# Padding two small tiles, a common ring for the spilled MLP blocks, and priorities for two short chains in a hybrid decoder layer

## The chip, the cores and the metric

The kernel runs on one core of one Trainium2 chip. A core has TensorE (PE in the profile; its weight loads are PEld), VectorE (DVE), ScalarE (ACT), GpSimd (POOL) and SyncE (SP), and 16 DMA engines; DMAs are issued by SP, ACT and POOL, each in the order of its own queue. The metric is the device time of one execution in microseconds.

## What is computed

One decoder layer on 512 rows of 1024 columns, all in float32. Cut to what matters:

```python
u = rms_norm(h, norm_mix_g)
conv_in, c_q, c_kv, k_rope_raw, gate_logits = split(u @ w_in)
conv_out = conformer_conv(conv_in, ...)           # 31 taps, layer norm, silu, @ w_conv_out
mla_out = mla_attention(c_q, c_kv, k_rope_raw, ...)  # rms_norm of both latents, 8 causal heads
gates = sigmoid(gate_logits)
h = h + (gates[0] * conv_out + gates[1] * mla_out) @ w_out
h = h + memory_cross_attention(rms_norm(h), rms_norm(mem), ...)
h = h + square(relu(rms_norm(h) @ w_mlp1)) @ w_mlp2
return rms_norm(h, final_norm_g)
```

## The kernel before

Every float32 operand of a product is split into a high part, rounded to the format `fp32r`, and a low rest, and a product is three: high by high, high by low, low by high (`mm3`, lines 237 to 239). `prep` makes the two parts of a weight block, `wh` on ScalarE (line 202) and `wl` on VectorE or GpSimd (line 203); a `Pipe` calls it one unit ahead of the products. Most products are 128x128 weights by 512 columns; in `w_mlp1`, `w_out`, `w_in` and the heads the moving operand is an activation (`hgh`, `mgh`, `uh`, `yh`, `cqh`) and the weights are `wh` and `wl`; in the second MLP product and for the values it is the other way round, and `hA`, `hB` or `ckh` or `mh` are loaded as the weights while `wh`, `wl` or `xh`, `xl` move.

The instructions of TensorE stay in the order of the code (`manual_schedule`). A planner orders those of the other engines when the program is built: it takes what is ready by its own clock, and among several the one traced first; `tc.high_priority()` moves the instructions of a block to the front of that choice.

The stages in order of time: convolution inputs (`ag`), the query latent (`cq`), gates 0 to 5, the key and value latent (`ckv`), gates 6 to 15; the convolution's 124 taps run on VectorE beside them (line 494). Then values and heads, `mla_out`, `w_out` with `mem_norm`, the memory's keys, queries and values, the cross-attention, `w_xo`; the first MLP product (`m1_unit`), 32 units; the second, in seven passes (`PASSES`) of four chunks with 24 products each: a Strassen scheme on halves of the rows and columns, for which blocks `a11` to `s4` are made beside the first product.

*Memory.* Tiles are put on two stacks in the on-chip memory, from the bottom (pools `cst`, `sm`, `w`, `g`, `hg`, `xa`, `o`, `m2`, ...) and from the top (`y`, `lat`, `u`, `att`, `h`, `xm`, `mg`, `mlp`, ..., those with `side="right"`). `cst` lies at the bottom, and `paced` (line 1364) is one of its tiles; `rm` (line 909) is one of `xm`'s. Nearly all larger tiles are whole multiples of 256 bytes in a partition, so a small one decides where all that come after it stand. In the compiled kernel `wh`, `wl`, `xh`, `xl`, `hgh`, `hgl`, `oh`, `xoh` and `xpt` begin 32 bytes past a multiple of 256; `uh`, `ul`, `cqh`, `yh`, `ckh`, `vh`, `q`, `k`, `hA` and `hB` 224; `mh`, `xkh`, `xvh` and `mgh` 160.

*Row factors.* `latent_rows` (line 673) takes the sums of squares of a latent's four row blocks, makes a factor for each row by `rsqrt` (12 short instructions on VectorE) and scales the rows out of the PSUM banks. Gates are evacuated by line 725 from the same kind of bank, `mm`, of which there are four; two hold a latent until it is scaled.

*Spilled blocks.* The blocks `s3` and `a22` (`SPILLED`) are written to DRAM by line 1250, each chunk after its four row blocks are made, and read back by `reload` on ScalarE's queue; the two names have two buffers each. `s3` is used in pass 5, `a22` in pass 6 (counted from 0).

Of the kernel before, what the change touches and what calls it, by code (L numbers as in the profile page):

```python
# [14 lines left out]
F32 = mybir.dt.float32  # L15
# [4 lines left out]
ALU = mybir.AluOpType  # L20
# [3 lines left out]
P = 128  # L24
D = 1024
S = 512
NT = S // P
# [12 lines left out]
EPS = 1e-6  # L40
# [128 lines left out]
def _body(tc, a):  # L169
    nc = tc.nc  # L170
    dma = nc.sync.dma_start
    pe = nc.tensor
    dve = nc.vector
    act = nc.scalar
    gps = nc.gpsimd

    def pool(name, bufs=1, side=None, space=None):
        kw = dict(name=name, bufs=bufs, reuse_waits="tile")
        if side:
            kw["side"] = side  # L180
        if space:
            kw["space"] = space
        cm = tc.tile_pool(**kw)
        return cm, cm.__enter__()
# [5 lines left out]
    cst_cm, cst = pool("cst")  # L190
    sm_cm, sm = pool("sm", bufs=2)
# [4 lines left out]
    def bank(tag="mm"):  # L196
        nonlocal ps
        return ps.tile([P, S], F32, tag=tag, name=tag, bufs=PB[tag])


    def split(hi, lo, src, eng=None):
        act.copy(hi, src)  # L202
        (eng or dve).tensor_tensor(lo, src, hi.bitcast(F32), op=ALU.subtract)  # L203

    def split_scaled(hi, lo, src, scale):
        act.activation(hi, src, AF.Copy, scale=scale)
        dve.scalar_tensor_tensor(lo, src, scale, hi.bitcast(F32), op0=ALU.mult, op1=ALU.subtract)
# [23 lines left out]
    def mm3(out, pairs, first=True, last=True, again=False):  # L231

        n = len(pairs)
        cols = out.shape[-1] / S
        for i, ((wh, wl), (ah, al)) in enumerate(pairs):
            kw = dict(skip_group_check=True) if again else {}
            pe.matmul(out, wh, ah, start=first and i == 0, stop=False, **kw)  # L237
            pe.matmul(out, wh, al, start=False, stop=False, **kw)  # L238
            pe.matmul(out, wl, ah, start=False, stop=last and i == n - 1, **kw)  # L239
            tick(cols)  # L240

    def rsqrt(dst, v, n):
        t = sm.tile([P, n], F32, tag="rs_t", name="rs_t")
        ti = sm.tile([P, n], I32, tag="rs_i", name="rs_i")
        dve.tensor_scalar(ti, v.bitcast(I32), 1, None, op0=ALU.logical_shift_right)
        dve.tensor_scalar(dst.bitcast(I32), ti, -1, 0x5F3759DF, op0=ALU.mult, op1=ALU.add)
        for _ in range(3):
            dve.scalar_tensor_tensor(t, dst, -0.5, dst, op0=ALU.mult, op1=ALU.mult)  # L248
            dve.tensor_tensor(t, t, v, op=ALU.mult)
            dve.scalar_tensor_tensor(dst, t, 1.5, dst, op0=ALU.add, op1=ALU.mult)  # L250
# [10 lines left out]
    rx = cst.tile([P, NT], F32, name="rx")  # L261
    rx2 = cst.tile([P, NT], F32, name="rx2")
# [71 lines left out]
    def lhs(hl, k, m0=0, m=128):  # L334
        return hl[0][:, k, m0:m0 + m], hl[1][:, k, m0:m0 + m]
# [97 lines left out]
    n = NT * 16  # L433
# [239 lines left out]
    def latent_rows(bs, dim, cn):  # L673
        ss = sm.tile([P, NT], F32, tag="ss", name="ss")
        for t in range(NT):
            junk = wkp.tile([P, S], F32, tag="sg", name="junk")
            act.activation(junk[:, :dim], bs[t][:, :dim], AF.Square, accum_out=ss[:, t:t + 1])
        v = sm.tile([P, NT], F32, tag="rv", name="rv")
        dve.scalar_tensor_tensor(v, ss, 1.0 / dim, rx2, op0=ALU.mult, op1=ALU.mult)
        dve.tensor_scalar(v, v, EPS, None, op0=ALU.add)  # L680
        r = sm.tile([P, NT], F32, tag="rr", name="rr")
        rsqrt(r, v, NT)
        dve.tensor_tensor(r, r, rx, op=ALU.mult)
        for t in range(NT):
            act.activation(cn[:, t, :dim], bs[t][:, :dim], AF.Copy, scale=r[:, t:t + 1])

# [68 lines left out]
    def qkt(tag):  # L755
        return at.tile([P, 2, S], F32R, tag=tag, name=tag, bufs=QB)
# [4 lines left out]
    def prep_q(p):  # L761
        return prep(("uq", p // 2), c0=256 * (p % 2), cols=256)

    def q_head(hl, h):
        b = bank()
        e = h % 2
        mm3(b, [(lhs(hl, k, 128 * e), (cqh[:, k, :], cql[:, k, :])) for k in range(3)])
        t = at.tile([P, S], F32, tag="qtmp", name="qtmp", bufs=1)
        dve.tensor_tensor(t, b, tq[:, e, :], op=ALU.mult)
        q = qkt("q")  # L770
        split(q[:, 0, :], q[:, 1, :], t)
        qs[h] = q
# [66 lines left out]
    hq = None  # L839
    k_pair(0)  # L840
    for t in range(NT):
# [3 lines left out]
        split(vh[:, t, :], vl[:, t, :], b)  # L845
        if t == 0:
            hq = prep_q(0)
    q_head(hq, 0)
    q_head(hq, 1)
    hqs = {0: hq}  # L850

# [48 lines left out]
    xm_cm, xmp = pool("xm", side="right")  # L900
# [5 lines left out]
    ml = xmp.tile([P, KD, MEM], F32R, name="ml")  # L906
    rbm = xmp.tile([P, MEM], F32, name="rbm")

    rm = xmp.tile([P, 16], F32, name="rm")
    mg_cm, mgp = pool("mg", side="right")  # L910
    mgh = mgp.tile([P, KD, S], F32R, name="mgh")
    mgl = mgp.tile([P, KD, S], F32R, name="mgl")
# [256 lines left out]
    HT = S // 2  # L1169
    ml_cm, mlp = pool("mlp", side="right")  # L1170
    hop_cm, hop = pool("hop")
    blocks = {}
# [11 lines left out]
    def block(name, c):  # L1184

        if (name, c) not in blocks:
            if name in SPILLED:
                blocks[name, c] = mlp.tile([P, 4, HT], F32, tag="sp_" + name, name="sp_" + name, bufs=2)
            else:
                t = pair_tile(name, c // 2, (2, 4))  # L1190
                blocks[name, c // 2 * 2], blocks[name, c // 2 * 2 + 1] = t[:, 0], t[:, 1]
        return blocks[name, c]


    SPILLED = ("s3", "a22")
    asp = {(n, c): spp.tile([P, 4 * HT], F32, name="%s_%d" % (n, c)) for n in SPILLED for c in range(4)}

    def reload(name, c):
        t = mlp.tile([P, 4, HT], F32, tag="sp_" + name, name="re_" + name, bufs=2)
        act.dma_start(out=t.rearrange("p k m -> p (k m)"), in_=asp[name, c])  # L1200
        blocks[name, c] = t

    m2w = {}
# [8 lines left out]
    def v3(t):  # L1212
        return t.rearrange("p (k m) -> p k m", k=4)
# [76 lines left out]
    def split_h(name, c):  # L1290
        hi = mlp.tile([P, 4, HT], F32R, tag="hA", name="hA", bufs=2)
        lo = mlp.tile([P, 4, HT], F32R, tag="hB", name="hB", bufs=2)
        src = block(name, c)
        if name == "a22":
            split_scaled(hi, lo, src, -1.0)
        else:
            split(hi, lo, src)
        return hi, lo

    def split_w(src):  # L1300
        out = []
        for u in range(2):
            w = whl4(2, S)
            split(w[0], w[1], src[:, 2 * u:2 * u + 2, :])
            out.append(w)
        return out
# [54 lines left out]
    def add_to(t, what, c):  # L1361
        gps.dma_start(out=t, in_=hbm(what, c), accum_op=ALU.add, max_dma_last_dim=8192)

    paced = cst.tile([P, 16], F32, name="paced")

    def pace(lo):

# [15 lines left out]
    def load_v(c):  # L1383
        vs[c] = flat(pair_tile(("a12", "s1")[c // 2], c % 2, (1, 1)))
        dma(out=vs[c], in_=hbm("b22", c))
# [87 lines left out]
    def pass_unit(n, c):  # L1473
        aname, bk, again = PASSES[n]
        end = n == len(PASSES) - 1

        def prep_():
            if aname in SPILLED:
                for cc in {0: (0, 1), 3: ()}.get(c, (c + 1,)):
                    reload(aname, cc)  # L1480
            src, nxt = w_source(n, c)
            h, w = split_h(aname, c), split_w(v3(src))
            if n == 0 and c >= 2:
                load_b21(c - 2)
            if n == 1 and c < 2:
                load_b21(2 + c)
            if n == 2:
                load_v(c)
            if nxt:
                add_to(src, nxt, c)  # L1490
            if n == 1:

                with tc.issue_after(pace(w[0][1])):
                    add_to(xs[c], "b12", c)
            return h, w

        def main(hw):
            h, w = hw
            if c == 0 and not again:
                acc_[bk] = [bank("at" if bk in "bd" else "mm") for _ in range(2)]  # L1500
            if end and c == 2:
                held["hw"] = hw
            elif end and c == 3:
                for t in range(2):
                    part(acc_[bk][t], t, *held["hw"], False, False, again)
                    part(acc_[bk][t], t, h, w, False, True, again)
                    DONE[n](t)
            elif c in (0, 3):
                for t in range(2):
                    part(acc_[bk][t], t, h, w, c == 0 and not again, c == 3, again)  # L1510
                    if c == 3:
                        DONE[n](t)
            else:
                chunk(acc_[bk], h, w, c, again)
            if n == 0 and c == 0:
                late_pools()
                load_x(3)
            if n == 2 and c == 0:
                m2w["gf"] = w_tile(m2w["p"], "b21", "gf")[:, :D]
                dma(out=m2w["gf"], in_=a["gfin"].to_broadcast([P, D]))  # L1520
        pipe.unit(prep_, main)
# [32 lines left out]
```

## Time and profile before

| | us |
|---|---|
| median of 3 runs | 774.58 (774.38 to 774.97) |
| the profiled execution | 775.09 |
| its span, first to last instruction | 773.2 |
| TensorE busy | 756.4 (98% of the span) |
| VectorE busy | 525.3 (68%) |
| ScalarE busy | 399.9 (52%) |
| GpSimd busy | 76.4 (10%) |
| granted clock of TensorE, mean | 0.997 of 2.4 GHz |

A row of a timeline gives an instruction's start and duration, its engine and line, the tiles it writes and reads (for a product: bank, moving operand, weights), shapes, how many, and in brackets how long the engine was idle before it and what ended that. The duration of a product includes its way through the array, so two products overlap; how fast they follow each other is read from their starts.

### The profile page before, as it was taken

To read this page: it belongs to the slowest core of one execution; us is meant where nothing else is said; L and a number is where in the kernel's file an instruction comes from. 1 tells how busy PE (TensorE), PEld (TensorE's weight loads), DVE (VectorE), ACT (ScalarE), POOL (GpSimd) and SP (SyncE) were. 2 spreads that over 40 slices of the span, in tenths; PEclk is the share of its full clock that TensorE was granted. 3 is DMA by queue.
4 is the path that set the end of the run, shared out by engine and by line. 5 is a ranking of instruction groups with operands and counts; after the bars stand their busy time and mean duration, and the time that the engine had idled before them with its cause. 6 is when DMAs were issued, how large, how long until landed. Compare 5 with 4: busy or idle time off the path is not lost.

```text
span 773.2 us, 9487 instructions
## 1 busy us (share of the span) xinstructions
PE 756.4 (98%) x3594; PEld 623.8 (81%) x3594; DVE 525.3 (68%) x855; ACT 399.9 (52%) x681; POOL 76.4 (10%) x64
## 2 busy tenths in 40 slices
PE   8999999999999999999999999999999999999896
PEld 5889788777788887889888888888888888888784
DVE  6899999845888859756686634233333567666895
ACT  7234333478667537344474635444344565656562
POOL 0144426320000000000000000000000011111000
PEclk9999999999999999999999999999999999999998
DMA  8323123222103144333321434334353499999731
GB/s 277 111 95 111 58 95 127 73 77 96 56 0 110 56 154 165 116 110 110 109 109 54 164 108 152 136 132 182 108 209 117 148 291 263 278 216 212 197 109 54
DMA packets 26989, 103.36 MB, mean 134 GB/s; under 512 B 2368, under 2 KB 9920, under 8 KB 17984
## 3 DMA queue, kind: packets, MB, share of 16 engines
q1 hardware_dynamic: 13600, 67.54, 24.4%
q0 software_dynamic: 2304, 16.78, 10.5%
q10 hardware_dynamic: 11040, 18.45, 6.8%
q8 instruction: 28, 0.46, 0.2%
q14 instruction: 17, 0.14, 0.1%
HBM read 94.37 MB, written 8.39 MB: 133 GB/s over the span
## 4 chain that ended last, share of the span: by engine, by line
PE 80%; DVE 13%; DMA 3%; ACT 2%; issue 1%; SPq 0%; DVEq 0%; ACTq 0%
PE mm L239 21%; PE mm L238 21%; PE mm L237 21%; DVE cv L494 6%; PE at L238 4%; PE at L237 3%; PE at L239 3%; DMA re_s<-s 1%; PE at L816 1%; DVE wl L203 1%; PE at L797 1%; DVE rs_t L248 1%; DMA xr<-xT 1%; PE at L798 1%; PE at L795 1%
## 5 line engine op out<-in xcount | busy, mean ns | idle before, releaser
L202 ACT CAST wh<-raw 128x1024 fp32r<-128x1024 f32 (+4 forms) x103 | 102.7, 998 | 176.9 <-PE mm L238 148.7
L203 DVE TENSOR_TENSOR wl<-raw,wh 128x1024 fp32r<-128x1024 f32 (+3 forms) x77 | 90.7, 1178 | 106.7 <-ACT wh L202 106.4
L237 PE MATMUL mm<-hgh,wh 128*128 128x512 f32 x288 | 113.1, 393 | 0.0
L239 PE MATMUL mm<-hgh,wl 128*128 128x512 f32 x288 | 112.3, 390 | 0.0
L238 PE MATMUL mm<-hgl,wh 128*128 128x512 f32 x288 | 112.2, 389 | 0.0
L494 DVE SCALAR_TENSOR_TENSOR cv<-zpad,vec,cv 128x512 f32<-128x512 f32 x116 | 80.4, 744 | 0.1
L237 PE MATMUL mm<-uh,wh 128*128 128x512 f32 x176 | 70.8, 402 | 1.8 <-DVE sg L725 1.8
L239 PE MATMUL mm<-uh,wl 128*128 128x512 f32 x176 | 69.6, 395 | 0.1
L238 PE MATMUL mm<-ul,wh 128*128 128x512 f32 x176 | 69.5, 395 | 0.0
L203 POOL TENSOR_TENSOR wl<-raw,wh 128x1024 fp32r<-128x1024 f32 (+2 forms) x26 | 56.4, 2169 | 107.7 <-ACT wh L202 102.9
L239 PEld LDWEIGHTS mm<-hgh,wl 128*128 128x128 f32 x288 | 54.1, 188 | 11.4
L237 PEld LDWEIGHTS mm<-hgh,wh 128*128 128x128 f32 x288 | 54.1, 188 | 10.9
L238 PEld LDWEIGHTS mm<-hgl,wh 128*128 128x128 f32 x288 | 54.1, 188 | 10.9
L1368 POOL COPY paced<-wl 128x1 f32<-128x1 f32 x4 | 2.5, 615 | 468.2 <-DVE wl L203 468.2
L203 DVE TENSOR_TENSOR wl<-x,wh 128x1024 fp32r<-128x1024 f32 x25 | 30.4, 1222 | 19.3 <-ACT wh L202 18.6
L237 PEld LDWEIGHTS mm<-uh,wh 128*128 128x128 f32 x176 | 33.0, 188 | 11.0 <-issue 3.8
L238 PE MATMUL at<-wl,hA 128*128 128x512 f32 x96 | 37.9, 395 | 2.4 <-DVE wl L203 2.4
L239 PEld LDWEIGHTS mm<-uh,wl 128*128 128x128 f32 x176 | 33.0, 188 | 8.5 <-DVE wl L203 0.6
L238 PEld LDWEIGHTS mm<-ul,wh 128*128 128x128 f32 x176 | 33.1, 188 | 7.3
L202 ACT CAST wh<-x 128x1024 fp32r<-128x1024 f32 x25 | 26.1, 1047 | 24.6 <-PE at L239 9.6
L237 PE MATMUL at<-wh,hA 128*128 128x512 f32 x96 | 37.6, 392 | 0.0
L239 PE MATMUL at<-wh,hB 128*128 128x512 f32 x96 | 37.4, 390 | 0.0
(392 smaller groups left out, 1717.3 us busy)
## 6 DMA issues: line engine op xcount, KB each, us to landing
raw<-weights SPq DMA_DIRECT2D x42, 1024.0 KB, 4.8
x<-weights POOLq DMA_DIRECT2D x12, 1024.0 KB, 14.7
a<-weights SPq DMA_DIRECT2D x5, 1024.0 KB, 9.7
x<-weights SPq DMA_DIRECT2D x4, 1024.0 KB, 5.1
raw<-weights SPq DMA_DIRECT2D x4, 768.0 KB, 4.2
xr<-xT SPq DMA_DIRECT2D x8, 256.0 KB, 6.2
raw<-weights SPq DMA_DIRECT2D x4, 512.0 KB, 5.0
ht<-xT ACTq DMA_DIRECT2D x1, 2048.0 KB, 9.2
```

Source lines behind the costliest of these rows:

```text
L202: act.copy(hi, src)
L203: (eng or dve).tensor_tensor(lo, src, hi.bitcast(F32), op=ALU.subtract)
L237: pe.matmul(out, wh, ah, start=first and i == 0, stop=False, **kw)
L238: pe.matmul(out, wh, al, start=False, stop=False, **kw)
L239: pe.matmul(out, wl, ah, start=False, stop=last and i == n - 1, **kw)
L248: dve.scalar_tensor_tensor(t, dst, -0.5, dst, op0=ALU.mult, op1=ALU.mult)
L494: dve.scalar_tensor_tensor(run if w < CW - 1 else acc[:, c, :], zs, wcol, run, op0=ALU.mult, op1=ALU.add)
L795: pe.matmul(b[:, :n], q[:, 0, sl], k[:, 0, :n], start=True, stop=False)
L797: pe.matmul(b[:, :n], q[:, 0, sl], k[:, 1, :n], start=False, stop=False)
L798: pe.matmul(b[:, :n], q[:, 1, sl], k[:, 0, :n], start=False, stop=True)
L816: pe.transpose(b[:, (t - k) * P:(t - k + 1) * P], ptok[h, t][:, k * P:(k + 1) * P], ident)
L1368: return gps.tensor_copy(paced[:, 0:1], lo[:, 0, 0:1].bitcast(F32)).ins
```

## The change

Two tiles of 16 columns become 64 columns wide. The row factors of a latent and the instructions of the first query head get priority. The blocks `s3` and `a22` share one ring of four buffers, and reloads are issued from SP: all four chunks of `s3` at the second chunk of pass 4, and a chunk of `a22` behind the split of each chunk of `s3` in pass 5.

```diff
--- before.py
+++ after.py
@@ -675,12 +675,14 @@
         for t in range(NT):
             junk = wkp.tile([P, S], F32, tag="sg", name="junk")
             act.activation(junk[:, :dim], bs[t][:, :dim], AF.Square, accum_out=ss[:, t:t + 1])
-        v = sm.tile([P, NT], F32, tag="rv", name="rv")
-        dve.scalar_tensor_tensor(v, ss, 1.0 / dim, rx2, op0=ALU.mult, op1=ALU.mult)
-        dve.tensor_scalar(v, v, EPS, None, op0=ALU.add)
-        r = sm.tile([P, NT], F32, tag="rr", name="rr")
-        rsqrt(r, v, NT)
-        dve.tensor_tensor(r, r, rx, op=ALU.mult)
+
+        with tc.high_priority():
+            v = sm.tile([P, NT], F32, tag="rv", name="rv")
+            dve.scalar_tensor_tensor(v, ss, 1.0 / dim, rx2, op0=ALU.mult, op1=ALU.mult)
+            dve.tensor_scalar(v, v, EPS, None, op0=ALU.add)
+            r = sm.tile([P, NT], F32, tag="rr", name="rr")
+            rsqrt(r, v, NT)
+            dve.tensor_tensor(r, r, rx, op=ALU.mult)
         for t in range(NT):
             act.activation(cn[:, t, :dim], bs[t][:, :dim], AF.Copy, scale=r[:, t:t + 1])
 
@@ -845,7 +847,8 @@
         split(vh[:, t, :], vl[:, t, :], b)
         if t == 0:
             hq = prep_q(0)
-    q_head(hq, 0)
+    with tc.high_priority():
+        q_head(hq, 0)
     q_head(hq, 1)
     hqs = {0: hq}
 
@@ -906,7 +909,7 @@
     ml = xmp.tile([P, KD, MEM], F32R, name="ml")
     rbm = xmp.tile([P, MEM], F32, name="rbm")
 
-    rm = xmp.tile([P, 16], F32, name="rm")
+    rm = xmp.tile([P, 64], F32, name="rm")
     mg_cm, mgp = pool("mg", side="right")
     mgh = mgp.tile([P, KD, S], F32R, name="mgh")
     mgl = mgp.tile([P, KD, S], F32R, name="mgl")
@@ -1185,7 +1188,7 @@
 
         if (name, c) not in blocks:
             if name in SPILLED:
-                blocks[name, c] = mlp.tile([P, 4, HT], F32, tag="sp_" + name, name="sp_" + name, bufs=2)
+                blocks[name, c] = mlp.tile([P, 4, HT], F32, tag="sp", name="sp_" + name, bufs=4)
             else:
                 t = pair_tile(name, c // 2, (2, 4))
                 blocks[name, c // 2 * 2], blocks[name, c // 2 * 2 + 1] = t[:, 0], t[:, 1]
@@ -1196,8 +1199,8 @@
     asp = {(n, c): spp.tile([P, 4 * HT], F32, name="%s_%d" % (n, c)) for n in SPILLED for c in range(4)}
 
     def reload(name, c):
-        t = mlp.tile([P, 4, HT], F32, tag="sp_" + name, name="re_" + name, bufs=2)
-        act.dma_start(out=t.rearrange("p k m -> p (k m)"), in_=asp[name, c])
+        t = mlp.tile([P, 4, HT], F32, tag="sp", name="re_" + name, bufs=4)
+        dma(out=t.rearrange("p k m -> p (k m)"), in_=asp[name, c])
         blocks[name, c] = t
 
     m2w = {}
@@ -1361,7 +1364,7 @@
     def add_to(t, what, c):
         gps.dma_start(out=t, in_=hbm(what, c), accum_op=ALU.add, max_dma_last_dim=8192)
 
-    paced = cst.tile([P, 16], F32, name="paced")
+    paced = cst.tile([P, 64], F32, name="paced")
 
     def pace(lo):
 
@@ -1475,11 +1478,13 @@
         end = n == len(PASSES) - 1
 
         def prep_():
-            if aname in SPILLED:
-                for cc in {0: (0, 1), 3: ()}.get(c, (c + 1,)):
-                    reload(aname, cc)
+            if n == 4 and c == 1:
+                for cc in range(4):
+                    reload("s3", cc)
             src, nxt = w_source(n, c)
             h, w = split_h(aname, c), split_w(v3(src))
+            if aname == "s3":
+                reload("a22", c)
             if n == 0 and c >= 2:
                 load_b21(c - 2)
             if n == 1 and c < 2:
```

## Rows read from the trace of the kernel before

**Rows 1.** The page: busy us (share of the span) and instructions of each engine.

```profile
PE 756.4 (98%) x3594; PEld 623.8 (81%) x3594; DVE 525.3 (68%) x855; ACT 399.9 (52%) x681; POOL 76.4 (10%) x64
```

**Rows 2.** Waits of TensorE: us in total, times, longest.

```profile
PE at L238 <- DVE wl L203: 2.4, 1, 2.4
PE mm L237 <- DVE sg L725: 1.8, 2, 1.0
...
PE at L795 <- ACT q L202: 1.0, 1, 1.0
```

**Rows 3.** Timeline, TensorE, first MLP product: start, us, line, tiles, [idle].

```profile
504.69 0.39 PE L238 MATMUL mm<-hgl,wh 128*128 128x512 f32 x1
...
505.85 0.39 PE L237 MATMUL mm<-hgh,wh 128*128 128x512 f32 x1
...
515.14 0.40 PE L239 MATMUL mm<-hgh,wl 128*128 128x512 f32 x1
```

**Rows 4.** Timeline, TensorE, gate products, first and last of 66 starts.

```profile
120.69 0.40 PE L238 MATMUL mm<-ul,wh 128*128 128x512 f32 x1
...
135.86 0.39 PE L237 MATMUL mm<-uh,wh 128*128 128x512 f32 x1
```

**Rows 5.** Timeline, TensorE, `w_out`, first and last of 71 starts.

```profile
311.69 0.40 PE L237 MATMUL mm<-mgh,wh 128*128 128x512 f32 x1
...
327.95 0.40 PE L238 MATMUL mm<-mgl,wh 128*128 128x512 f32 x1
```

**Rows 6.** Timeline, TensorE, memory values, first and last of 30 starts.

```profile
393.13 0.40 PE L237 MATMUL mm<-wh,mh 128*128 128x512 f32 x1
...
399.87 0.39 PE L239 MATMUL mm<-wh,ml 128*128 128x512 f32 x1
```

**Rows 7.** Table of stretches: us, busy us (instructions) by engine, clock, DMA share, GB/s.

```profile
33.20:120.20 87.00, 85.94 (x440) 74.38 (x439) 86.98 (x141) 31.76 (x56) 36.57 (x18) 1.00 0.24 84
120.60:137.40 16.80, 16.11 (x70) 12.64 (x68) 16.76 (x29) 4.33 (x7) 9.56 (x12) 1.00 0.36 126
640.00:728.00 88.00, 88.00 (x386) 72.23 (x385) 61.92 (x66) 49.79 (x58) 11.49 (x14) 1.00 1.01 239
```

**Rows 8.** Timeline, VectorE, around the two latents.

```profile
74.53 0.35 DVE L679 SCALAR_TENSOR_TENSOR rv<-ss,rx 128x4 f32<-128x4 f32 x1
74.80 0.74 DVE L494 SCALAR_TENSOR_TENSOR cv<-zpad,vec,cv 128x512 f32<-128x512 f32 x1
...
77.65 2.11 DVE L248 SCALAR_TENSOR_TENSOR rs_t<-rr 128x4 f32<-128x4 f32 x1
...
88.02 0.68 DVE L725 TENSOR_TENSOR sg<-mm,rbx 128x512 f32<-128x512 f32 x1
...
120.64 0.31 DVE L679 SCALAR_TENSOR_TENSOR rv<-ss,rx 128x4 f32<-128x4 f32 x1 [0.46 <-ACT junk L677]
...
136.63 0.68 DVE L725 TENSOR_TENSOR sg<-mm,rbx 128x512 f32<-128x512 f32 x1
```

**Rows 9.** Timeline, VectorE, row factors of `mem_norm`.

```profile
310.50 0.15 DVE L248 SCALAR_TENSOR_TENSOR rs_t<-rm 128x2 f32<-128x2 f32 x1
310.57 0.48 DVE L207 SCALAR_TENSOR_TENSOR ml<-mr,vec,mh 128x256 fp32r<-128x256 f32 x1
310.96 0.15 DVE L249 TENSOR_TENSOR rs_t<-rs_t,rv 128x2 f32<-128x2 f32 x1
```

**Rows 10.** Timeline, VectorE, first query head.

```profile
194.38 1.23 DVE L203 TENSOR_TENSOR wl<-raw,wh 128x1024 fp32r<-128x1024 f32 x1 [0.39 <-ACT wh L202]
195.52 0.69 DVE L769 TENSOR_TENSOR qtmp<-mm,tq 128x512 f32<-128x512 f32 x1
```

**Rows 11.** Timeline, ScalarE, third `s3` chunk.

```profile
715.51 0.33 ACTq L1200 DMA_DIRECT2D re_s<-s  x1
...
726.89 1.05 ACT L202 CAST hA<-re_s 128x1024 fp32r<-128x1024 f32 x1 [3.09 <-DMA re_s<-s]
```

**Rows 12.** Timeline, VectorE, third `s3` chunk.

```profile
727.98 1.23 DVE L203 TENSOR_TENSOR hB<-re_s,hA 128x1024 fp32r<-128x1024 f32 x1 [1.89 <-ACT hA L202]
```

## The prediction

> **What bounds the kernel now.** I read the page first: TensorE has work in 756.4 of 773.2 us, 98% [rows 1]. So a gain has to come from one of two places: TensorE standing still, or its products following each other more slowly than they could. The list of waits gives the first: 2.4 us once on `wl`, 1.8 us in two pieces on `sg`, 1.0 us on `q` [rows 2], about 5 us in all; what else it holds is small or in the start-up. The second I read in the timeline from the starts of consecutive products of one shape (128x128 weights, 512 columns). In the first MLP product 41 intervals from 505.85 to 515.14 us make 9.29 us, 0.2266 us each [rows 3]. In the gate products 65 make 15.17, 0.2334 each [rows 4]; in `w_out` 70 make 16.26, 0.2323 [rows 5]; in the memory values 29 make 6.74, 0.2324 [rows 6]; in the second MLP product 386 starts in 88 us, two of them cut by the edges, make 0.229 [rows 7]. The granted clock is 1.00 in that window and in two others [rows 7], and 0.997 over the run, so the clock is not the difference.
>
> What differs is the place of the two operands in a 256-byte line. In the compiled kernel before, the left stack (`wh`, `wl`, `xh`, `xl`, `hgh`, `hgl`, `oh`, `xoh`, `xpt`) stands 32 bytes past a line, the right stack (`uh`, `cqh`, `yh`, `ckh`, `vh`, `hA`) 224, the `xm` pool and what lies on it (`mh`, `mgh`, `xvh`) 160. Equal places: 0.2266. Moving operand at 224, weights at 32: 0.2334. Moving at 32, weights at 224: 0.229. And 128 bytes apart: 0.2323 with the moving operand at 160, 0.2324 with the weights at 160. That these two agree is what I lean on most: 128 ahead and 128 behind are the same only if the line of 256 bytes decides. All three places straddle lines alike, so an absolute alignment would not sort them.
>
> One more thing is in rows 3: after four transposes five intervals, 504.69 to 505.85, take 1.16 us, 0.232 each, and only then does the pace settle. Equal places need some products to settle, so short runs gain less.
>
> **The change part by part.** *The two pads.* `paced` from 64 to 256 bytes moves everything on the left that is allocated after `cst` by 192: 32 becomes 224. `rm` from 64 to 256 bytes makes the pool `xm` a whole number of lines, so 160 becomes 224. All wide operands then stand at 224. No instruction is added. By stage, with counts from the code:
> - Gates after the second latent: units 9 to 15, 7 x 24 products x 0.0068 = 1.1 us.
> - Heads: values 24, `k_pair` 24, `q_head` 72, `conv_out` 96 products, x 0.0068 = 1.5 us at most; but they run in sixes to twelves between transposes, where equal places too are at 0.232 [rows 3]. Ends 0 and 1.5; I take 0.7, since about half of a run of twelve is settled.
> - `w_out` 192, memory values and outputs 72 products, x 0.0057 = 1.5 us, less the unsettled starts: 1.3.
> - Second MLP product: 7 passes x 4 chunks x 24 = 672, x 0.0024 = 1.6 us; I take 1.5. VectorE and ScalarE are busy in 61.92 and 49.79 of the 88 us [rows 7], so they can follow.
> - Products of 256 columns after 137 us, 144 of them: nothing shows them at equal places. At 0.0024 either way they are worth 0.3; taken as 0.
>
> That is 4.6 us. *Before 137 us the same pads gain almost nothing.* From 33.2 to 120.2 us VectorE is busy in 86.98 of 87.00 us, and from 120.6 to 137.4 in 16.76 of 16.80 [rows 7]. Its order is fixed when the program is planned. The first factor of the second latent, at 120.64, comes after only 0.46 us of idle time, and the gate evacuation behind that chain, at 136.63 [rows 8], is one of the two that TensorE waits for [rows 2]. A TensorE that is faster by some 2 us (336 products x 0.0068) arrives earlier and waits longer; 0.5 us is left. So the pads give 5.1 us.
>
> A page of the Trainium skill speaks against the pads: "TensorE: Matmul & The Clock Gate", Part 2, in its step by step, gives TensorE two independent read ports and says that loading the next weights takes nothing from the running matmul. By that rule the place would not matter and the sum would be 1.9 us; the trace, with 0.2266 beside 0.2334 at one clock [rows 3, 4], does not agree with it.
>
> *Priority for the row factors.* In the first latent the first factor starts at 74.53, behind taps, and from there factors and taps alternate [rows 8]. Taps that were traced earlier stand before it; there priority helps, by a few taps of 0.74 us. The alternation is not a matter of priority: in `mem_norm` the factors are traced before the splits, and still one split goes between two of them [rows 9], because the next factor isn't ready when VectorE comes free. So the chain starts earlier but stays as long, and the evacuation behind it, at 88.02 [rows 8], keeps the same taps before it. TensorE may then take the latent's own bank instead and wait less there (one piece of the 1.8 us of rows 2), but VectorE, full to 120.2, collects the debt at 137. I take 0. The ends are -2 and +2 us: one more or one fewer of the factors that last 2.11 us instead of a fraction [rows 8].
>
> *Priority for the first query head.* `qtmp` at 195.52 stands behind a `wl` at 194.38 [rows 10] of 1024 columns. The queries' weights have 768, so it belongs to `w_conv_out`, which is traced later. It has the lower priority already and went first because `qtmp` was not ready in the plan; raising the head changes nothing: 0. At best the 1.0 us of rows 2; at worst the same again, if the weights pushed back are late.
>
> *One ring of four, reloads on SP.* Before, chunks 2 and 3 of `s3` wait for a buffer: a reload goes out at 715.51, once chunk 0 is split, and `hA` starts at 726.89 after 3.09 us on that DMA [rows 11]. In the new ring all four `s3` chunks can lie there early: two buffers come free with the spills of chunk 2 and two with those of chunk 3, as many early transfers as before (two `s3`, two `a22`). Each `a22` chunk follows once its `s3` chunk is split, a whole pass ahead of its use, some 22 us against the 11.4 that the crowded transfer took. So that wait goes. What is late next is VectorE: it idles 1.89 us before `hB` at 727.98 [rows 12], and the instructions of `finish` around it are closely packed. So 1.9 of the 2.4 us comes back; ends 1.5 and 2.4. SP has nothing behind the late reloads but the last output rows. The early ones stand between weight loads on SP; if one holds a load up, that costs at worst the 3.09 us that the late reload cost ScalarE here. I take 0, because a weight load has a whole chunk in reserve.
>
> **Sum.** 5.1 + 0 + 0 + 1.9 = 7.0 us. The profiled execution took 775.09 us (span 773.2), 0.51 above the median of 774.58; the sum taken off gives 768.1 and 767.6. I predict 767.6.
>
> **The rivals.**
> *The place does not matter.* The pace then belongs to the stages, and only the reload pays: 774.58 - 1.9 = 772.7. For it: place and stage go together everywhere. Against: three stages of different load at 0.2323 to 0.2334 and two orders of the same two tiles' places at one pace. Chance 0.05. (The skill's rule above would end here.)
> *Left with right stays slow.* No settled run of right with right is in the trace, and after the change the left stack and `uh`, `cqh`, `hA` are an odd number of 256-byte lines apart; if 512 bytes are the measure, they stand half of it apart. `xm`, with `rm` at 256 bytes, does not: `w_out` and the memory values still gain 1.3. 774.58 - 1.9 - 1.3 = 771.4, and 770 to 773 with the unknown pace. Against: rows 5 and 6 agree. Chance 0.13.
> *The place 224 itself is slow.* Then the products that are fast now, both operands at 32, lose what the gate products show: 768 of `w_mlp1` and 288 of `w_xq`, `w_xo` and `w_mla_out`, x 0.0068 = 7.2 us; less 1.9 that is 779.9. It decides in the first MLP product: from some 280 products at 0.2334 on, the reload is outweighed. For it: both pairs with 224 are slower than both at 32. Against: they are not alike, 0.229 and 0.2334. Chance 0.10.
> *As forecast*: 0.72, with the bounds above 764 to 770.
>
> **How the numbers follow.** The range 764.0 to 772.6 holds nearly all of the forecast's case (0.68) and most of the second rival (0.12). About 0.2%, 1.55 us, is what a measurement of this kernel can tell from no change, so faster means below 773.0: 0.70 from the forecast, 0.03 and 0.09 from the first two rivals, 0.82. Same 0.07, slower 0.11.
>
> **What would show it.** Right: starts 0.2266 us apart in the gates, `w_out` and the passes, and still so in `w_mlp1`; no wait of TensorE near 730; a longer wait on `sg` near 87 or 137. Wrong: starts at 0.229 to 0.234 where left meets right; `w_mlp1` above 0.23; or a gain before 137 us, which would mean that VectorE's order or its 2 us instructions changed.

## The result, and the profile after

The changed kernel takes 768.06 us (median of 4 runs, 767.29 to 768.86), the kernel before beside it 774.48 (774.18 to 774.97): 0.9917 of the time, 95% interval 0.9899 to 0.9934. The prediction was 767.6, range 764.0 to 772.6, so it was right, and most of its steps held. Three didn't come out as told: the reload was worth more, the priority at the latents cost something, and TensorE's clock took 1.5 us back in the profiled execution (768.86 us, span 767.1).

The page's line of busy time, and of TensorE's waits the largest (us in total, times, longest):

```profile
PE 751.9 (98%) x3594; PEld 625.3 (82%) x3594; DVE 524.9 (68%) x855; ACT 400.0 (52%) x681; POOL 77.4 (10%) x64
PE mm L237 <- DVE rr L250: 1.6, 1, 1.6
...
PE at L797 <- ACT q L202: 1.1, 1, 1.1
PE mm L237 <- DVE sg L727: 0.9, 1, 0.9
...
PE mm L237 <- ACT cnq L687: 0.6, 1, 0.6
```

Against [rows 1, 2]: TensorE is busy 4.5 us less for the same 3594 instructions. The wait on the reload (`wl`, 2.4 us) is gone, that on `q` stands. Near the first latent one wait on `sg` became waits on `rr` and on `cnq`.

Timeline of TensorE (start, us, line, tiles): a run of gate products and one of `w_out` with the transpose behind it. Then the table of stretches (busy us and instructions of PE, PEld, DVE, ACT, POOL, then clock, DMA share, GB/s).

```profile
119.37 0.40 PE L237 MATMUL mm<-uh,wh 128*128 128x512 f32 x1
...
135.51 0.39 PE L239 MATMUL mm<-uh,wl 128*128 128x512 f32 x1
...
305.97 0.40 PE L239 MATMUL mm<-mgh,wl 128*128 128x512 f32 x1
...
328.65 0.38 PE L271 MATMUL at<-kon,rm 128*128 128x128 f32 x2
```

```profile
33.20:120.20 87.00, 84.79 (x440) 74.38 (x439) 87.00 (x140) 32.08 (x58) 36.67 (x19) 1.00 0.24 84
120.60:137.40 16.80, 15.90 (x71) 12.87 (x70) 16.80 (x29) 4.50 (x8) 9.13 (x10) 1.00 0.37 126
640.00:728.00 88.00, 88.00 (x390) 72.88 (x389) 66.03 (x74) 53.61 (x62) 12.40 (x14) 1.00 1.01 243
```

The gates' 71 intervals in 16.14 us are 0.2273 each, their unsettled first ones included [rows 4: 0.2334]; `w_out`'s 100 in 22.68 us are 0.2268 [rows 5: 0.2323]; in the passes 390 starts fit where 386 did [rows 7], 0.2268 instead of 0.229. All three now have the pace of the first MLP product [rows 3], whose own is unchanged. VectorE is as full before 137 us as it was.

When the n-th product of both traces is set side by side, the difference of the starts is the gain so far. By place in the trace before:

| gain so far, us | 47 us | 134 | 198 | 262 | 296 | 403 | 602 | 726 | 732.5 | 765 |
|---|---|---|---|---|---|---|---|---|---|---|
| after | 0.90 | 0.76 | 1.53 | 0.63 | 0.70 | 1.72 | 1.71 | 2.85 | 5.47 | 6.10 |
| pads alone | 0.38 | 0.56 | 1.33 | 2.03 | 2.11 | 2.82 | 2.86 | 4.00 | 3.95 | 2.55 |
| ring alone | -0.14 | -0.13 | -0.14 | -0.15 | -0.14 | -0.36 | -0.36 | -0.36 | 2.23 | 2.57 |
| priorities alone | -0.06 | -0.92 | -0.92 | -0.93 | -0.93 | -1.00 | -1.01 | -1.01 | -0.77 | -2.40 |
| pads and ring, no priorities | 0.58 | 0.79 | 1.57 | 2.27 | 2.35 | 3.38 | 3.37 | 4.51 | 7.13 | 7.76 |

The other rows are experiments below. At 29.7 us, ahead of the first long run of products, the gain of after is 0.44, of pads alone -0.10 and of the last row 0.10: that is start-up, which differs by some tenths from execution to execution. From there to 81 us each of the three gains 0.9 us by the pace, and by 90 us the waits at 82 and 88 us have taken nearly all of it back: the gains are 0.28, -0.06 and 0.16.

The kernel after loses 1.5 us between 198 and 201 us of its own time. The stretches of TensorE there (busy us and instructions, clock, DMA share, GB/s), and the first scores with the wait ahead of them:

```profile
195.38 0.33 PE L797 MATMUL at<-k,q 128*128 128x128 f32 x1 [1.06 <-ACT q L202]
```

```profile
194.00:196.00 2.00, 0.83 (x5) 1.00 0.00 0
196.00:198.00 2.00, 1.90 (x12) 0.88 0.01 4
198.00:200.00 2.00, 2.00 (x6) 0.50 0.29 41
200.00:202.00 2.00, 2.00 (x8) 0.76 0.90 344
202.00:206.00 4.00, 4.00 (x20) 1.00 0.17 70
```

The granted clock falls from 1.00 to 0.50, 2.4 to 1.2 GHz, for some three us, shortly after TensorE stood still for 1.06 and 0.21 us behind `q`; 6 products fit where 10 would. The kernel before had nearly the same wait there [rows 2, 10] and no such fall in its trace.

### The profile page after: what moved, and what is told of

Read it like the earlier page. It is cut to its first block, busy times and chain, and to the rows that moved or that the text cites. A ratio compares the mean times of both kernels' runs of the same rounds, so it can differ in the third digit from the quotient of the medians.

```text
span 767.1 us, 9493 instructions
## 1 busy us (share of the span) xinstructions
PE 751.9 (98%) x3594; PEld 625.3 (82%) x3594; DVE 524.9 (68%) x855; ACT 400.0 (52%) x681; POOL 77.4 (10%) x64
## 4 chain that ended last, share of the span: by engine, by line
PE 79%; DVE 16%; ACT 2%; issue 1%; DMA 1%; SPq 0%; DVEq 0%; ACTq 0%
PE mm L239 20%; PE mm L237 20%; PE mm L238 20%; DVE cv L494 9%; PE at L239 4%; PE at L238 4%; PE at L237 4%; PE at L818 1%; PE at L799 1%; DVE wl L203 1%; DMA xr<-xT 1%; DVE sg L727 1%; PE at L800 1%; PE at L797 1%; DVE mt L927 1%
```

## Experiments

All times are medians; the kernel before took 774.57 to 774.91 beside them.

| kernel | us | lowest to highest |
|---|---|---|
| pads alone | 772.10 | 769.82 to 775.79 |
| ring alone | 772.31 | 771.90 to 772.94 |
| priorities alone | 775.83 | 774.94 to 778.18 |
| after, all operands at 32 | 767.22 | 766.82 to 767.86 |
| after, left stack 128 further | 775.00 | 774.65 to 775.29 |
| after, left stack 64 back | 773.18 | 772.76 to 773.99 |
| after without priorities | 767.13 | 767.11 to 767.25 |
| after, third head early | 766.32 | 766.03 to 766.51 |
| after, taps at rate 0.68 | 774.43 | 773.59 to 775.28 |
| no priorities, third head early | 765.98 | 765.67 to 766.39 |
| the same, row factors on GpSimd | 762.34 | 762.17 to 763.03 |

### The parts one by one

**The pads alone** (before, with this edit; the order of instructions on every engine is that of before):

```diff
-    rm = xmp.tile([P, 16], F32, name="rm")
+    rm = xmp.tile([P, 64], F32, name="rm")
-    paced = cst.tile([P, 16], F32, name="paced")
+    paced = cst.tile([P, 64], F32, name="paced")
```

> The kernel before with the two pads alone; the order of instructions on every engine is that of before. Theory (equal places pay): all 512-column products settle at 0.2267 us; the time falls by 5.1 us by the prediction, 4.9 by the trace of after (2.85 gained up to 726 us, 1.5 lost to the low clock near 199 added back, 0.6 after 733): 769.4 to 769.8, or 771 in executions where the clock falls near 199 us too. Rival (the pace belongs to the stages or to the new orders): 774.5. The wait on the reload near 727 stays, 2 to 3 us.

By the trace 4.00 us are gained up to 726 us, so the place pays with nothing else changed. The median, 772.1, is above the forecast, and only the lowest run, 769.82, comes up to it. The trace shows what happened in the profiled execution (772.54 us): the wait on the reload, and then the stretches of TensorE behind it.

```profile
728.55 0.50 PE L238 MATMUL at<-wl,hA 128*128 128x512 f32 x1 [2.51 <-DVE wl L203]
```

```profile
728.00:730.00 2.00, 1.45 (x5) 0.82 0.50 184
730.00:732.00 2.00, 2.00 (x7) 0.50 0.00 0
732.00:734.00 2.00, 2.00 (x9) 0.83 0.01 1
734.00:736.00 2.00, 2.00 (x11) 1.00 0.74 259
```

Again a wait and then the clock at 0.50. The gain falls from 3.95 us to 2.55 over the last stretch, where after gained 0.63. The other runs fit, though they were not traced: the three quickest, up to 770.69 us, have a mean granted clock of 0.997 to 0.998, this one 0.995, the three slowest, from 773.57 us on, 0.993. One of 773.00 us has 0.998, so the clock is not all of the spread.

**The ring and the reloads on SP alone** (of the change's diff all that belongs to `sp`, `reload` and `prep_`, no pads, no priorities):

```diff
-    ... tag="sp_" + name, name="sp_" + name, bufs=2)
+    ... tag="sp", name="sp_" + name, bufs=4)
-        act.dma_start(out=t.rearrange("p k m -> p (k m)"), in_=asp[name, c])
+        dma(out=t.rearrange("p k m -> p (k m)"), in_=asp[name, c])
```

> The kernel before with the ring of four and the reloads on SP alone. Prediction: 1.9 us less, 772.6. Trace of after: 2.6 us less, 771.9, because VectorE's order around the second low half is planned anew. Rival (the wait moves to VectorE or to a weight load behind the early reloads): 0 to 0.5 us less, 774 or more.

2.3 us less by the medians, and by the trace 2.59 us between 726 and 732.5 us. No wait of TensorE is left between 720 and 740 us. VectorE's timeline shows why the whole wait went and not 1.9 us of it:

```profile
721.47 1.22 DVE L203 TENSOR_TENSOR hB<-re_s,hA 128x1024 fp32r<-128x1024 f32 x1
...
724.60 1.22 DVE L203 TENSOR_TENSOR wl<-s,wh 128x1024 fp32r<-128x1024 f32 x1
...
727.33 1.21 DVE L203 TENSOR_TENSOR hB<-re_s,hA 128x1024 fp32r<-128x1024 f32 x1
```

The `hB` that came at 727.98 [rows 12] comes 0.65 us earlier, and the `wl` that TensorE waited for has been moved ahead of instructions of `finish`: the program is planned anew when a transfer is expected earlier.

**The two priorities alone:**

```diff
+        with tc.high_priority():
             v = sm.tile([P, NT], F32, tag="rv", name="rv")
...
+    with tc.high_priority():
         q_head(hq, 0)
```

> The kernel before with the two priorities alone. Prediction: 0, between 772.5 and 776.5 at its ends: 774.5. Rival A (the priority is what gained before 137 us): the time falls by 0.5 to 0.8, 773.8. Rival B (the priority brings the low clock near 199 us): the granted clock falls to 0.5 for some 3 us shortly after 194 us and the time rises by 1.5, 776.

775.83 against 774.64 us; the recorded ratio is 1.0005 (0.9990 to 1.0019), too little to call. The traces tell more. VectorE of the kernel before, then of the priorities alone, then TensorE of the latter:

```profile
81.14 0.68 DVE L725 TENSOR_TENSOR sg<-mm,rbx 128x512 f32<-128x512 f32 x1
87.95 0.15 DVE L683 TENSOR_TENSOR rr<-rr,rx 128x4 f32<-128x4 f32 x1
```

```profile
73.30 1.61 DVE L681 SCALAR_TENSOR_TENSOR rv<-ss,rx 128x4 f32<-128x4 f32 x1
...
82.65 0.68 DVE L727 TENSOR_TENSOR sg<-mm,rbx 128x512 f32<-128x512 f32 x1
88.00 0.15 DVE L685 TENSOR_TENSOR rr<-rr,rx 128x4 f32<-128x4 f32 x1
```

```profile
83.47 0.47 PE L237 MATMUL mm<-uh,wh 128*128 128x512 f32 x1 [1.48 <-DVE rr L250]
89.77 0.50 PE L237 MATMUL mm<-uh,wh 128*128 128x512 f32 x1 [0.45 <-ACT cnq L687]
```

The chain starts 1.2 us earlier and ends no earlier, 88.00 for 87.95. But an evacuation of the gates, `sg`, which stood behind seven factors, now stands behind nine, 1.5 us later, and its bank is what TensorE waits for (the list names `rr`, which ends just after that `sg`, but a gate product reads no factor). Of the 1.45 us lost there 0.6 come back at 88 us; 0.9 stays to the end. Near 195 us nothing changes in the trace, so rival B of the expectation is out. The further loss at the end, -0.77 to -2.40, is for the most part the clock at 0.50 about the end of the reload's wait, as with the pads alone. Some 0.3 us of it is the pace: the 64 products from 736.69 us on, behind the low clock, follow each other at 0.2333 us, where these passes have 0.2289 otherwise.

**After without the priorities** (the two lines of the last diff taken out of after).

> The kernel after without the two priorities: pads, ring and reloads alone. The prediction put the priorities at 0; the kernel with the priorities alone lost 0.9 us at the first latent. If that holds beside the pads, 0.9 us less than after without its low clock near 199 us, 766.5; if the latent's chain only takes over the wait that VectorE owes anyway, the same as after, 767.3 to 768.9. No wait on rr at 82 us; waits on sg near 87 and 137 in its place, about 2 us together.

767.13, within 0.14 us in five runs. The waits are as expected, and a third of 0.9 us on `rs_t`. The quicker two executions of after are at 767.29 and 767.37, so beside the pads the priorities cost 0.2 us by the times here and 0.34 in the pair 766.32 and 765.98 below, both little against the scatter. The traces show it better: from 29.7 to 134 us this kernel gains 0.38 us more than after, and that other pair differs by 0.33. From ring alone to this kernel the medians fall by 5.18 us, and by 5.45 when each is set against the kernel before beside it (774.64 and 774.91): that is what the pads are worth where no wait on a reload disturbs.

### Which measure of place it is

**Everything at 32 in the line.**

```diff
+    rp_cm, rp = pool("rp", side="right")
+    rp.tile([P, 48], F32, name="rpad")
     y_cm, yp = pool("y", side="right")
...
-    paced = cst.tile([P, 64], F32, name="paced")
+    paced = cst.tile([P, 16], F32, name="paced")
```

> The kernel after, but with all wide operands at 32 in the 256-byte line instead of 224: the left stack back where it was before, the right stack moved by a 192-byte tile that nothing uses. Theory (only the difference of the two places counts): every pace as in after, 0.2267 us, and 767.3 to 768.9. Rival (224 itself is a good place, or the pad on the left is): left with left back to something slower than 0.2267 in the first MLP product, 1056 products, 771 or more.

767.22 us, and 390 starts in 88 us of the passes, as in after:

```profile
640.00:728.00 88.00, 88.00 (x390) 1.00 1.00 243
```

So neither 224 nor the pad on the left counts, but that the places are equal.

**Half a line apart**, and **64 bytes apart the other way round** (after, each with one line changed):

```diff
-    paced = cst.tile([P, 64], F32, name="paced")
+    paced = cst.tile([P, 96], F32, name="paced")
...
+    paced = cst.tile([P, 48], F32, name="paced")
```

> The kernel after with the left stack 128 bytes further on, at 96 in the 256-byte line, the right stack and the memory's pool at 224: left with right are now half a line apart, left with left still at equal places. Theory (only the difference of the places modulo 256 counts, and half a line costs what it cost w_out before, 0.2323 to 0.2324): gates and second MLP product both at 0.2323, so the gates are quicker than in the kernel before (0.2334) and the passes slower (0.229), w_out at 0.2323, w_mlp1 at 0.2267. Some 1250 products by 0.0057 make 7.1 us more than after, 775 us. Rival (the pace belongs to the stage or to the absolute place): gates and passes at their paces of before or of after, 768 to 773 us.

> The kernel after with the left stack at 160 in the 256-byte line (64 bytes less than the pad of after), the right stack and the memory's pool at 224. The moving operand of the gates now stands 64 bytes ahead of its weights, as that of the passes did in the kernel before (32 against 224 is 64 ahead over the line's end), and the passes' moving operand 64 bytes behind, as the gates' did before. Theory (difference of the places modulo 256): the two paces change over, gates 0.229, second MLP product 0.2334, w_out and memory values 0.229, w_mlp1 0.2267; 672 x 0.0067 and some 450 x 0.0023 make 5.6 us more than after without its low clock, 773 us. Rival (the stage or the absolute place has its pace): gates 0.2334 and passes 0.229, or all at 0.2267.

TensorE half a line apart: gates, and the stretch of the passes.

```profile
120.53 0.39 PE L237 MATMUL mm<-uh,wh 128*128 128x512 f32 x1
...
137.03 0.40 PE L239 MATMUL mm<-uh,wl 128*128 128x512 f32 x1
```

```profile
640.00:728.00 88.00, 88.00 (x380) 1.00 1.01 240
```

64 bytes the other way: two runs of gates, and the passes.

```profile
119.86 0.40 PE L237 MATMUL mm<-uh,wh 128*128 128x512 f32 x1
...
136.19 0.40 PE L238 MATMUL mm<-ul,wh 128*128 128x512 f32 x1
...
137.87 0.39 PE L238 MATMUL mm<-ul,wh 128*128 128x512 f32 x1
...
148.40 0.40 PE L239 MATMUL mm<-uh,wl 128*128 128x512 f32 x1
```

```profile
640.00:728.00 88.00, 88.00 (x379) 1.00 0.99 236
```

Half a line apart, gates (71 intervals in 16.50 us) and passes (380 starts in 88 us, two of them cut by the edges) are both at 0.2324 to 0.2328, the gates quicker and the passes slower than before; 775.00 us as forecast. Not all products obey: the first two long runs of this kernel, 151 products up to 81 us with the same distance, are still at 0.2333. With the order of the places turned round, the passes take the gates' old pace, 0.2334, and the gates mostly the passes' old one: 46 intervals from 137.87 us in 10.53, 0.2289; 773.18 us as forecast. One run of the gates doesn't obey: 70 intervals from 119.86 us in 16.33, 0.2333. The memory values, which the expectation put at 0.229, are at 0.2331 in 36 intervals from 390.30 us; there the weight block is the moving operand, so it stands 64 bytes behind as in the passes, and a pace like theirs is what the distance asks for. The stage has no pace of its own; that rival is out.

### What limits TensorE before 137 us, and a quicker kernel

**The third query head's products ahead of the first scores:**

```diff
+    hqs[1] = prep_q(1)
+    q_head(hqs[1], 2)
     scores(0)
-    proj(2)
+    k_pair(1)
     hco = prep_co(0)
```

> The kernel after with the third query head's products ahead of the first head's scores, nine products of 0.227 us as cover for the split of q. Theory: the wait of 1.06 us on q near 195 us goes, and with it the low clock that follows it near 199 us: 766.2 to 766.6, and no executions 1.5 us apart from the rest. Rival (the weights of the second pair, now split earlier, come late): a wait of about 1 us on wl or qtmp in the same place, 767.5 to 769.

766.32 us, four runs within 0.5. The first scores start without a wait, and no stretch near them has a low clock:

```profile
196.63 0.22 PE L797 MATMUL at<-k,q 128*128 128x128 f32 x1
```

**Taps at a lower rate:**

```diff
-TAP_RATE = 0.75
+TAP_RATE = 0.68
```

> The kernel after with the convolution's taps at 0.68 instead of 0.75 per product group, so that VectorE's taps reach to about 157 us instead of 147 and it isn't full before 137 us. Theory (the pads can gain nothing before 137 us because VectorE is full): VectorE gets idle time there, the waits on rr, sg and cnq, 3.1 us together, shrink to 1 us or less, and the time falls by about 2 us to 765.5 to 766.5. Rival (the waits come from the length of the factor chain, not from VectorE's load, or the later end of the convolution delays the heads): 767.3 or more.

774.43 us: the theory's forecast missed, the second half of the rival came true (the heads are late), and the experiment doesn't test the theory. VectorE's stretch, and a wait of TensorE later on:

```profile
33.20:120.20 87.00, 84.85 (x440) 74.47 (x439) 87.00 (x140) 31.33 (x54) 36.84 (x18) 1.00 0.24 84
```

```profile
195.91 0.47 PE L237 MATMUL mm<-wh,ckh 128*128 128x512 f32 x1 [3.42 <-DVE k L203]
```

VectorE is as full as ever, and the last tap starts at 147 us in both kernels. The rate sets when taps are traced, and that didn't change when they run. What moved is the layer norm traced behind them, with new waits of TensorE on `ln` and `acc` from 182 to 187 us, and the heads came late; behind the wait of 3.42 us the clock falls to 0.50 here too. So whether VectorE's load or the length of the factor chain makes TensorE wait stays open here.

**No priorities, third head early; and the same with the latents' row factors on GpSimd**, but for the two integer steps, which stay on VectorE:

```diff
-        dve.scalar_tensor_tensor(v, ss, 1.0 / dim, rx2, op0=ALU.mult, op1=ALU.mult)
-        dve.tensor_scalar(v, v, EPS, None, op0=ALU.add)
+        gps.tensor_tensor(v, ss, rx2, op=ALU.mult)
+        gps.tensor_scalar(v, v, 1.0 / dim, EPS, op0=ALU.mult, op1=ALU.add)
...
+        for _ in range(3):
+            gps.tensor_tensor(t, r, r, op=ALU.mult)
+            gps.tensor_tensor(t, t, v, op=ALU.mult)
+            gps.tensor_scalar(t, t, -0.5, 1.5, op0=ALU.mult, op1=ALU.add)
+            gps.tensor_tensor(r, r, t, op=ALU.mult)
+        gps.tensor_tensor(r, r, rx, op=ALU.mult)
```

> Pads, ring and reloads, without the two priorities, and with the third query head's products ahead of the first head's scores. Theory (the priority at the latents costs up to 0.5 us, the early head brings 0.9): 765.8 to 766.3. Rival (the wait at the first latent only moves to 137 us, so the priorities are worth nothing beside the pads): 766.3, as with the priorities.

> As the kernel without priorities and with the early third head, and the latents' row factors on GpSimd, but for the two integer steps. Theory (before 137 us TensorE goes by VectorE's fixed and full order): some 13 us of factors, with four of 2 us, leave VectorE, it gets idle time before 137 us, the waits on sg and rs_t there, 3 us together, go, and the time falls by 2 to 3 us, 763.3 to 764.3. Rival (GpSimd's steps stand behind its own splits of 2.4 us, so the chain is longer): waits on cnq and cnk of some us, 766 to 770.

765.98 and 762.34 us. The second is 0.9838 of the time before (0.9819 to 0.9858) and the best kernel here. Its stretches before 137 us, and two of GpSimd's factors:

```profile
33.20:120.20 87.00, 87.00 (x453) 77.00 (x452) 83.30 (x130) 33.02 (x58) 42.61 (x42) 1.00 0.26 87
120.60:137.40 16.80, 16.80 (x75) 13.64 (x74) 16.80 (x25) 5.67 (x9) 12.39 (x18) 1.00 0.26 95
```

```profile
75.83 0.20 POOL L687 TENSOR_TENSOR rs_t<-rr 128x4 f32<-128x4 f32 x1 [1.33 <-DVE rr L685]
...
79.18 0.20 POOL L691 TENSOR_TENSOR rr<-rr,rx 128x4 f32<-128x4 f32 x1
```

TensorE has no wait left in either stretch, 87.00 of 87.00 and 16.80 of 16.80 us, and VectorE has 3.70 us of idle time in the first. In the second VectorE is as full as ever, and still TensorE doesn't wait: a full VectorE alone is not what held it up. The factors leave VectorE and their chain gets shorter in one edit, so the run doesn't tell which of the two pays. Against the kernel without this edit, products near 156 us start 3.2 us earlier. The rival was wrong: the 13 factors of this run on GpSimd, 75.83 to 79.18, take 0.2 us each, and the chain ends at 79 us where it ended at 88 in the kernel before.

## Why the prediction was right, point by point

**The pace goes by the difference of the operands' places in a 256-byte line.** Shown for equal against unequal places: with all at 224 or all at 32 every long run settles at 0.2267 to 0.2268. Which of the slower paces a distance gives is shown less strictly: with the distances set anew the paces of gates and passes change over, but a few runs took another pace, as said. Left with right stand an odd number of 256-byte lines apart in after and still have the pace, so the rival of 512 bytes is wrong, and so are the other two. The Trainium skill, "TensorE: Matmul & The Clock Gate", Part 2, step by step, says that loading the next weights takes no SBUF read bandwidth from the running matmul. What the prediction drew from it, that the place doesn't matter, the runs contradict: pads alone gained 4.00 us by 726 us. Whether it is the two reads that disturb each other was not shown; the runs show the pace, not its cause inside the engine.

**The pads' 5.1 us.** Measured 5.18 by the medians. By stage, from the table's last row, against the prediction: before 134 us 0.79 (0.10 of it start-up) for 0.5; to 198 us 0.78 for 1.1; heads 0.78 for 0.7; `w_out` to the first MLP product 1.02 for 1.3; passes 1.77 (1.14 to 726 us, 0.63 after 732.5) for 1.5. So the sum is right partly because its errors cancel. The claim that little of the gain before 137 us is kept held: without the priorities TensorE's waits near 82, 88 and 137 us grew to 3.0 us in all, and of the 0.9 us that the pace had gained by 81 us nearly nothing was left at 90. That it is VectorE's order which takes it fits, since taking the row factors off VectorE is what gave 3.2 us there; that it does so by being full is not shown.

**Priority for the row factors: 0.** The step that was off. The chain starts earlier and factors and taps still alternate. In priorities alone its end doesn't move, as said; beside the pads it ends 1.0 us earlier, 86.78 for 87.81 without the priorities, but two more taps then stand ahead of the next evacuation. What was left out is who stands between: an evacuation passed by two factors. It costs 0.9 us alone and 0.2 to 0.4 beside the pads, inside the ends of 2 us. VectorE around the first latent of after, to be read against [rows 8]:

```profile
72.79 0.99 DVE L681 SCALAR_TENSOR_TENSOR rv<-ss,rx 128x4 f32<-128x4 f32 x1
...
76.55 2.02 DVE L248 SCALAR_TENSOR_TENSOR rs_t<-rr 128x4 f32<-128x4 f32 x1
...
81.43 0.68 DVE L727 TENSOR_TENSOR sg<-mm,rbx 128x512 f32<-128x512 f32 x1
...
86.78 0.15 DVE L685 TENSOR_TENSOR rr<-rr,rx 128x4 f32<-128x4 f32 x1
86.86 1.40 DVE L494 SCALAR_TENSOR_TENSOR cv<-zpad,vec,cv 128x512 f32<-128x512 f32 x2
88.17 0.68 DVE L727 TENSOR_TENSOR sg<-mm,rbx 128x512 f32<-128x512 f32 x1
```

The chain begins 1.74 us earlier than in the kernel before, two factors still take 2 us (at 76.55 and 84.22), and the `sg` that comes after it is at 88.17 for 88.02.

**Priority for the first head: 0.** Right: `wl` of 1024 columns and then `qtmp` come in the same order as [rows 10], and the wait on `q` is 1.06 us for 1.0. It took other work in that place, the third head, to remove it.

**Ring and reload: 1.9.** The mechanism was right, the term too small: 2.6 us (ring alone 2.59, and 2.62 from 726 to 732.5 us in after). The prediction kept VectorE's order and let it be late next; that order was planned anew. The early reloads on SP held up no weight load that TensorE would have waited for.

**The sum.** 7.0 forecast; measured 6.10 at the last product with the low clock, and some 7.6 without it (1.5 lost near 200 us added back). The two executions of after at 767.3 and the two at 768.8 are 1.5 us apart, as much as the trace loses there. Only one was traced, but the mean granted clock of both at 768.8 is 0.996 and that of the other two 0.997, which fits. That the median lies only 0.5 us from the forecast is in part luck: the reload's 0.7 us more, the priorities' cost and a low clock in two of four executions nearly cancel.

## What to carry to other kernels

Look at where the two operands of a product begin within a 256-byte line; when starts of equal products are some per cent apart in different stages at one clock, a pad of some bytes in front of a stack may bring them together, and costs no instruction. Ahead of an engine whose queue is full, as VectorE's was here, a priority exchanges places: ask whose evacuation the raised steps will pass, and rather move small dependent steps to an engine that stands idle. And test each part alone, since a part that costs can hide in a sum that comes out right.

## What was not expected of the hardware

**Paces are few, and a run of products keeps one.** Beside 0.2267 runs of 24 and more products settled near 0.2289, 0.2323 and 0.2334 only, and a run that had settled kept its pace. Equal places gave 0.2267 after a few products in every traced run. Unequal ones gave mostly one pace for a distance, but not always. With 64 bytes turned round all runs of the gates had 0.2289 but one, 71 products at 0.2333; half a line apart the first 151 products had 0.2333 and the later ones 0.2323; and in priorities alone 64 products of the passes had 0.2333 for 0.2289. What picks the pace of a run was not found.

**The clock falls after a wait in some executions only.** 0.50 was granted for about three us after TensorE's wait of 1.27 us at 195 us in two pieces (after), 2.51 at 728 (pads alone) and 3.42 at 196 (taps at the lower rate), and from the end of its wait of 2.19 at 733 (priorities alone), but not after 2.42 at 732 in the trace of before, nor after the same 1.27 us in the kernel with all at 32 or in that without priorities. The mean granted clock of each run points the same way: of the 23 runs of the kernel before beside the first experiments six have 0.995, and take 776.33 to 778.43 us; the other 17 have 0.996 to 0.999 and take 773.30 to 776.54. Beside that stands that kernels without a wait on a reload agree within 0.1 to 1.7 us over their runs, and those with it spread over 3 to 6 in twelve runs or more, though only one run of each was traced. So a wait can cost more than its length; what decides was not settled.

**VectorE's short factors of 2 us end with GpSimd's splits.** In after the `rs_t` of 2.02 us ends at 78.57 us, and this is GpSimd beside it:

```profile
76.16 2.39 POOL L203 TENSOR_TENSOR wl<-raw,wh 128x1024 fp32r<-128x1024 f32 x1 [2.40 <-ACT wh L202]
```

It ends at 78.55. The same holds for all six factors of the two latents in after that last 0.99 to 2.24 us: each starts beside a split of 2.4 us that is under way and ends within 0.03 us of it. The taps, whose running sum lies in a PSUM bank, keep 0.74 us beside such a split (three of them from 90.81 us on, beside the one from 90.53 to 92.94). On GpSimd, in the quickest kernel, the step corresponding to that `rs_t` takes 0.20 us. The Trainium skill, "SBUF — State Buffer", section "Who interferes with whom", says that a VectorE instruction with two inputs in SBUF contends with a GpSimd instruction that reads SBUF, and that the one that comes second waits until the first is done; this trace agrees. One of the six factors, `rr` from `rs_i` at 122.79 us, has a single input and took 2.24 us all the same.
